# Gated linear attention inside a two-layer hybrid trunk: decay levels by products, one group of coupling products, full-size output products

## The chip, the cores and the metric

The kernel runs on one core of one Trainium2 chip. The metric is the device time of one execution in microseconds (us), as the median of several runs. TensorE is called PE in the profile (its weight loads PEld), VectorE DVE, ScalarE ACT, GpSimd POOL, SyncE SP. SP issues all transfers here.

## The reference, cut to what matters

A trunk of two layers over 2048 tokens of width 1024, all in float32. Each layer projects its input once and splits the columns between four heads of a gated delta rule (DeltaNet, "dn") and four heads of gated linear attention (GLA). Both groups are normalised by head, multiplied by a SiLU gate path, joined, projected back and added to the input before a layer norm. The change is in the GLA part, which computes, for keys of 64 channels and values of 128:

```python
# S_t = diag(exp(gk_t)) S_{t-1} + k_t v_t^T,   o_t = S_t^T q_t
log_f = jax.nn.log_sigmoid(gate_logits) / GLA_TAU          # GLA_TAU = 16, per token and key channel
Bc = jnp.cumsum(gc, axis=-2)                               # running log decay in a chunk
dec = jnp.where(causal, jnp.exp(diff), 0.0)                # diff = B_i - B_j, i >= j
attn = jnp.einsum("bhnid,bhnjd,bhnijd->bhnij", qc, kc, dec)
# over chunks:
o_n = einsum(q_n * exp(b_n), S) + einsum(a_n, v_n)
S = S * exp(b_last)[..., None] + einsum(k_n * exp(b_last - b_n), v_n)
```

The couplings `attn` can't be one matrix product, since the decay depends on the key channel too; and `q exp(B)` times `k exp(-B)` over a whole chunk would overflow.

## The kernel before

The work is done by layer and by half of the sequence (1024 tokens), so four times over. In each half the tokens come in two blocks of 512 (`b`), each of four chunks of 128 (`c`). Heads of GLA go in pairs (`p`): two heads of 64 key channels fill the 128 partitions, and `h` is the head in the pair. So there are four GLA blocks in a half, called (p, b) here, and 16 in all. DeltaNet has four heads by two blocks, eight blocks a half, numbered `n`.

A half runs in this order: transposes of the input (`prep_xt`) and token-major value projection (`proj_v`); the decay gates; the GLA blocks, with the projections for the next one (`gla_load`) between them; the DeltaNet keys (`keys_of`, `dn_keys`) one block ahead of the rest (`dn_rest`, which calls `dn_merge`); the gate paths (`gate`) strewn in between; the output projection with layer norm (`out_proj`). Projections (`proj_group`, L176 to L179) are products of 128 x 128 by 512 columns in a float32 form that is split in a high and a low part; 24 of them make one group of 128 channels for one block. The small products of GLA and DeltaNet are plain float32, each of which the profile counts as two instructions.

The order on each engine is fixed ahead of time by a scheduler that goes by priority (program order) and by its own estimate of durations; `issue_after` and `keep_in_program_order` are hints to it. Buffers come by tag, and a table (`SLOTS`, `BANKS`) says how many there are of each. Of the eight PSUM banks two are for projections ("pj"), three for transposes and couplings ("tr"), two for outputs ("ch") and one for merges ("mg").

The GLA block (`gla_block`) gets q and k, channels first, and the running log decay B from `gla_gates`, which sums it with a scan for each chunk (L331). To keep exponents small, it takes the couplings in levels: at level s, tokens of the second half of each stretch of 2s meet keys of the first half, both scaled by the decay to the border between the halves. Every level has its own subtraction from B, two exponentials on ACT and products on DVE. The levels 64, 32 and 16 (`LEVELS_BLOCK`) give whole blocks of the coupling matrix (L400); base blocks of 32 x 32 without decay come from L373; the levels 8, 4, 2 and 1 (`LEVELS_MASK`) come as 32 x 32 blocks, of which a mask picks the right entries (L439, L443). For these, q is laid out in a tile padded with zeros (`qpad`), so that one product with a contraction of 128 gives both heads. Then, chunk by chunk, an output product with the couplings A (L467, contraction 128), one with the state S (L468, contraction 64), the sum of squares on ACT, a copy on DVE, and the product that renews the state (L471), with the state itself on DVE (L472). `run_later` puts the transposes of the finished heads (`finish_head`) of the block before into the middle of the next.

SiLU and the exponentials need different tables on ACT. The gates of the first GLA head (`gla_gate(0)`) and the keys of DeltaNet's block 0 take a tanh form (`by_tanh`). DeltaNet's decay matrices (`dn_decay`) are exponentials too; they are written to DRAM and read back by `dn_keys`.

Of the kernel before, what the change touches and what calls it, by code (L numbers as in the profile page):

```python
# [9 lines left out]
F32 = mybir.dt.float32  # L10
# [3 lines left out]
ALU = mybir.AluOpType  # L14
# [15 lines left out]
SLOTS = {"xt": 4, "wh": 3, "wl": 3, "wr": 2, "oT": 10, "kT": 3, "kd": 3, "dec": 2, "U": 2, "Nn": 2, "lf": 2, "g4": 4,  # L30
# [8 lines left out]
def hymba_trunk(ctx: ExitStack, tc, x, w_in, conv_w, dn_a_log, dn_dt_bias, gla_gate_w2, gla_gate_b,  # L39
# [45 lines left out]
    # masks of the 32 x 32 diagonal blocks of the GLA couplings  # L85
# [21 lines left out]
    # starting rows of the triangular inversions: row 4 g + r of an identity at partition (g, chunk, block)  # L107
# [20 lines left out]
    cwh = C([P, 48], "cwh")  # L128
# [31 lines left out]
    later, anchor, tables = [], [], []  # L160
# [42 lines left out]
    def layer_params(l):  # L203
# [6 lines left out]
        nc.vector.tensor_scalar(out=cwh, in0=cw, scalar1=0.5, scalar2=None, op0=ALU.mult)  # L210
# [81 lines left out]
    def dn_decay(cums, n, decd):  # L292
        """Decay matrix of a block, transposed: exp(G_i - G_j) at [j, i], j <= i, with G the running log decay."""
# [6 lines left out]
        for c in range(NC):  # L300
            i = (b * NC + c) * 4 + h
            r = nc.scalar.activation(d[:, c, :], d[:, c, :], AF.Exp, bias=ngc[:, i:i + 1])
# [48 lines left out]

    def gla_block(p, qk, B, v, S):
        it = 1.0 / TAU
        qT, kT = qk
        B3 = B.rearrange("p (c t) -> p c t", c=NC)

        QE = T([P, BLK], "vb")
        EB = T([P, BLK], "y")
        anchor.append(nc.scalar.activation(EB, B, AF.Exp, scale=it))
        nc.vector.tensor_tensor(out=QE, in0=qT, in1=EB, op=ALU.mult)  # L360
        edec = small(NC, "edec")
        nc.vector.tensor_copy(edec, EB.rearrange("p (c t) -> p c t", c=NC)[:, :, P - 1])

        A = T([P, NC, 2, P], "g4")
        nc.gpsimd.memset(A, 0.0)
        banks = [PS([P, BLK], "tr") for _ in range(2)]
        d32 = [t[:, 0:256].rearrange("p (k c i) -> p k c i", k=2, c=NC) for t in banks]
        d64 = [t[0:64, 256:512].rearrange("p (c i) -> p c i", c=NC) for t in banks]
        for c in range(NC):
            for h in range(2):  # L370
                for j in range(0, P, 32):
                    r, cs = slice(64 * h, 64 * h + 64), slice(c * P + j, c * P + j + 32)
                    nc.tensor.matmul(d32[h][j:j + 32, 0, c, :], kT[r, cs], qT[r, cs], start=True, stop=True)  # L373

        def level(s):
            n = BLK // (2 * s)
            w = T([P, 515], "raw")[:, 0:BLK]
            w3 = w.rearrange("p (n t) -> p n t", n=n)
            Bn = B.rearrange("p (n t) -> p n t", n=n)
            nc.vector.tensor_tensor(out=w3, in0=Bn, in1=Bn[:, :, s - 1:s].to_broadcast([P, n, 2 * s]),  # L380
                                    op=ALU.subtract)
            nc.scalar.activation(w3[:, :, 0:s], w3[:, :, 0:s], AF.Exp, scale=-it)
            nc.scalar.activation(w3[:, :, s:], w3[:, :, s:], AF.Exp, scale=it)
            lv = T([P, BLK], "y")
            l3 = lv.rearrange("p (n t) -> p n t", n=n)
            nc.vector.tensor_tensor(out=l3[:, :, 0:s], in0=w3[:, :, 0:s],
                                    in1=kT.rearrange("p (n t) -> p n t", n=n)[:, :, 0:s], op=ALU.mult)
            nc.vector.tensor_tensor(out=l3[:, :, s:], in0=w3[:, :, s:],
                                    in1=qT.rearrange("p (n t) -> p n t", n=n)[:, :, s:], op=ALU.mult)
            return lv  # L390

        for s in LEVELS_BLOCK:
            lv = level(s)
            for c in range(NC):
                for h in range(2):
                    r = slice(64 * h, 64 * h + 64)
                    for j in range(0, P, 2 * s):
                        dst = (d64[h][:, c, :] if s == 64 else d32[h][j:j + s, 1, c, :] if s == 32
                               else d32[h][j:j + s, 0, c, s:])
                        nc.tensor.matmul(dst, lv[r, c * P + j:c * P + j + s], lv[r, c * P + j + s:c * P + j + 2 * s],  # L400
                                         start=True, stop=True)
        run_later()
        Ad = T([P, NC, 2, 32], "Y")
        for h in range(2):
# [5 lines left out]
        for s in LEVELS_MASK:  # L410
            n = BLK // (2 * s)
            q3 = qT.rearrange("p (n t) -> p n t", n=n)[:, :, s:]
            Bn = B.rearrange("p (n t) -> p n t", n=n)
            w = T([P, 515], "raw")[:, 0:BLK]
            if s > 1:
                w3 = w.rearrange("p (n t) -> p n t", n=n)
                nc.vector.tensor_tensor(out=w3, in0=Bn, in1=Bn[:, :, s - 1:s].to_broadcast([P, n, 2 * s]),
                                        op=ALU.subtract)
                nc.scalar.activation(w3[:, :, 0:s], w3[:, :, 0:s], AF.Exp, scale=-it)
                nc.scalar.activation(w3[:, :, s:], w3[:, :, s:], AF.Exp, scale=it)  # L420
                e3 = w3[:, :, s:]
                nc.vector.tensor_tensor(out=w3[:, :, 0:s], in0=w3[:, :, 0:s],
                                        in1=kT.rearrange("p (n t) -> p n t", n=n)[:, :, 0:s], op=ALU.mult)
# [30 lines left out]
        for c in range(NC):  # L454
            nc.tensor.transpose(pt[:, c, :], KE[:, c * P:(c + 1) * P], ident)
# [475 lines left out]
```

## Time and profile before

| | |
|---|---|
| median of 3 runs | 2501.54 us (2499.32 to 2502.89) |
| profiled execution, first to last instruction | 2508.8 us; no other time of that execution is listed |
| busy: PE, DVE, ACT, POOL | 2363.1, 1725.3, 1113.4, 327.6 us |
| mean granted PE clock | 0.964 |
| memory traffic | 157.84 MB read, 37.81 MB written |

The stages below are cut by hand at the lines that begin them: in the first half the GLA stage is 45 to 235 us from the start of the span and the DeltaNet stage 235 to 530; output projection and the next input follow to 665. A line of a group or of the timeline names the line of the kernel, the engine, the operation, the tile written and the tiles read, and the sizes. Matmuls overlap in the pipeline, so their lengths add up to more than the time that passes; the distance between two starts is what one costs. In tables by stretch of time each engine has its busy time and, in brackets, its instructions, and the last three columns are granted PE clock, DMA share and GB/s.

### The profile page before, as it was taken

The numbers are of one execution on the slowest core, as the hardware profiler recorded it, in microseconds if no ns is written. First come the engines' busy times: TensorE is split into PE (matmuls) and PEld (weight loads), VectorE is DVE, ScalarE is ACT, GpSimd is POOL, SyncE is SP. The second block draws the span as 40 slices with busy tenths as digits, with TensorE's granted clock in tenths as the row PEclk, the third lists the DMA queues.
The fourth block names the chain that finished last, engine by engine and source line by source line (L and its number), as shares of the span: only waits on it lengthen the run. The fifth ranks groups of instructions, "written<-read, shape, count | busy, mean of one in ns | idle before, by whom it ended". The sixth has DMA issues, their size and how long they took to land. (4 is left out here: it accounts for less than half of the span.)

```text
span 2508.8 us, 47498 instructions
## 1 busy us (share of the span) xinstructions
PE 2363.1 (94%) x17970; PEld 1891.7 (75%) x17970; DVE 1725.3 (69%) x4728; ACT 1113.4 (44%) x3149; POOL 327.6 (13%) x629
## 2 busy tenths in 40 slices
PE   8999999999999999989999989999999999999998
PEld 7776777788877677768887767777888877777777
DVE  4557777785556777777565678787766567777775
ACT  4654444451465444445146544444415654444440
POOL 2101111110010121111001012111100101211100
PEclk9999898999999999999999999999999999999999
DMA  4312121343321122144332122214433211222242
GB/s 140 83 35 68 50 74 33 94 148 101 117 70 53 50 60 65 34 99 144 102 118 69 53 51 60 65 37 105 145 99 116 78 45 42 64 60 54 75 133 80
DMA packets 242988, 198.72 MB, mean 79 GB/s; under 512 B 51972, under 2 KB 195656, under 8 KB 242760
## 3 DMA queue, kind: packets, MB, share of 16 engines
q1 hardware_dynamic: 242760, 195.70, 27.3%
q8 instruction: 141, 2.31, 0.4%
q14 instruction: 87, 0.71, 0.1%
HBM read 157.84 MB, written 37.81 MB: 78 GB/s over the span
## 5 line engine op out<-in xcount | busy, mean ns | idle before, releaser
L176 PE MATMUL pj<-xt,wh 128*128 128x512 f32 x1536 | 639.9, 417 | 2.0 <-ACT wh L152 2.0
L177 PE MATMUL pj<-xt,wh 128*128 128x512 f32 x1536 | 637.2, 415 | 0.0
L179 PE MATMUL pj<-xt,wl 128*128 128x512 f32 x1536 | 463.1, 424 | 0.0
L176 PEld LDWEIGHTS pj<-xt,wh 128*128 128x128 f32 x1536 | 298.4, 194 | 56.6 <-ACT wh L152 2.9
L177 PEld LDWEIGHTS pj<-xt,wh 128*128 128x128 f32 x1536 | 299.2, 195 | 54.9 <-issue 2.2
L179 PEld LDWEIGHTS pj<-xt,wl 128*128 128x128 f32 x1536 | 286.5, 198 | 53.1 <-issue 2.3
L490 DVE SCALAR_TENSOR_TENSOR y<-raw,cw,y 128x512 f32<-128x512 f32 x276 | 205.1, 743 | 29.0 <-ACT y L488 27.5
L745 PE MATMUL pj<-xt,wh 128*128 128x512 f32 x512 | 200.9, 392 | 0.0
L746 PE MATMUL pj<-xt,wh 128*128 128x512 f32 x512 | 200.3, 391 | 0.0
L152 ACT CAST wh<-wr 128x1024 fp32r<-128x1024 f32 (+2 forms) x116 | 118.6, 1023 | 158.5 <-PE pj L746 88.3
L154 DVE TENSOR_TENSOR wl<-wr,wh 128x1024 fp32r<-128x1024 f32 (+2 forms) x116 | 137.6, 1189 | 68.3 <-ACT wh L152 54.4
L698 POOL TENSOR_TENSOR ssd<-ssd,mhalf 128x1 f32<-128x1 f32 x128 | 87.1, 680 | 505.4 <-DVE ssd L697 505.0
L579 DVE TENSOR_TENSOR tmp<-Tb,g 128x64 f32<-128x64 f32 (+6 forms) x224 | 138.3, 617 | 3.0
L247 PE MATMUL pj<-wh,xt 128*128 128x280 f32 (+1 forms) x512 | 136.4, 297 | 0.0
L248 PE MATMUL pj<-wl,xt 128*128 128x280 f32 (+1 forms) x512 | 134.6, 294 | 0.9 <-issue 0.9
L748 PE MATMUL pj<-xt,wl 128*128 128x512 f32 x512 | 129.5, 391 | 0.0
L746 PEld LDWEIGHTS pj<-xt,wh 128*128 128x128 f32 x512 | 96.4, 188 | 19.2
L745 PEld LDWEIGHTS pj<-xt,wh 128*128 128x128 f32 x512 | 96.2, 188 | 19.2
L748 PEld LDWEIGHTS pj<-xt,wl 128*128 128x128 f32 x512 | 95.6, 188 | 19.2
L248 PEld LDWEIGHTS pj<-wl,xt 128*128 128x128 f32 x512 | 98.4, 192 | 2.0 <-issue 1.8
L247 PEld LDWEIGHTS pj<-wh,xt 128*128 128x128 f32 x512 | 98.4, 192 | 1.3 <-issue 0.7
L737 ACT CAST wh<-oT 128x128 fp32r<-128x128 f32 x128 | 30.2, 295 | 149.3 <-PE pj L746 140.4
(247 smaller groups left out, 4470.4 us busy)
## 6 DMA issues: line engine op xcount, KB each, us to landing
wr<-in_w_in_dram SPq DMA_DIRECT2D x104, 512.0 KB
g<-nd SPq DMA_DIRECT2D x32, 512.0 KB
g<-in_w_out_dram SPq DMA_DIRECT2D x32, 512.0 KB
g<-in_x_dram SPq DMA_DIRECT2D x16, 512.0 KB
dec<-gr SPq DMA_DIRECT2D x32, 256.0 KB
decd<-dec SPq DMA_DIRECT2D x32, 256.0 KB
dec<-decd SPq DMA_DIRECT2D x32, 256.0 KB
og<-oT SPq DMA_DIRECT2D x32, 256.0 KB
```

What stands on the lines that cost most here:

```text
L152: nc.scalar.copy(hi, raw)
L154: nc.vector.tensor_tensor(out=lo, in0=raw, in1=hi.bitcast(F32), op=ALU.subtract)
L176: nc.tensor.matmul(acc, hi[:, k, :], xh[:, k, :], start=(k == 0), stop=False)
L177: nc.tensor.matmul(acc, hi[:, k, :], xl[:, k, :], start=False, stop=False)
L179: nc.tensor.matmul(acc, lo[:, k, :], xh[:, k, :], start=False, stop=(k == KT - 1))
L247: nc.tensor.matmul(acc, xh[:, k, cs], ws[k][0], start=(k == 0), stop=False)
L248: nc.tensor.matmul(acc, xh[:, k, cs], ws[k][1], start=False, stop=False)
L490: nc.vector.scalar_tensor_tensor(out=y, in0=raw[:, k:k + BLK], scalar=w[:, 12 * k + grp:12 * k + grp + 1], in1=y, op0=ALU.mult, op1=ALU.add)
L579: nc.vector.tensor_tensor(out=tmp, in0=Tb[:, :, 0:w].unsqueeze(2).to_broadcast([P, 4, 4, w]), in1=NbT[:, w:w + 4, 0:w].unsqueeze(1).to_bro ...
L745: nc.tensor.matmul(acc, oh[:, k, :], wh[:, k, :], start=(k == 0), stop=False)
L746: nc.tensor.matmul(acc, oh[:, k, :], wl[:, k, :], start=False, stop=False)
L748: nc.tensor.matmul(acc, ol[:, k, :], wh[:, k, :], start=False, stop=(k == KT - 1))
```

## The change

It has five parts.

- `gla_gates` gives the forget factors f themselves (one more exponential) and no running sums. `span_decays` multiplies neighbours on POOL, so that `spans[s]` holds the decay over each stretch of s tokens. The levels are carried on: keys and queries scaled for level 2s come from those of level s, half of them multiplied by a span (DVE), the other half copied (ACT). The last step gives QE and KE, and `spans[128]` the chunk decay.
- All coupling products and the products that renew the state are issued after the last level, in one chain of order. The levels 8 to 1 are taken for one head at a time, with a contraction of 64. The states of all four chunks are worked out ahead (`Sall`).
- QE is a tile of two zero-padded halves, so that the product with the state has a contraction of 128. All 16 output products of a block come in a row, into two banks; squares and scaled copies are read from there.
- The tanh forms go away. One table load for SiLU is placed behind the last decay exponential, and every SiLU behind it; each decay exponential is placed behind the last.
- The second gate of GLA and the keys of DeltaNet's block 0 change places around the last GLA block. The gated outputs of the first two DeltaNet heads go to DRAM as well, and `split_o` reads six heads from there instead of four.

```diff
-SLOTS = {... "oT": 10, ... "g4": 4,
+SLOTS = {... "oT": 6, ... "g4": 4, "tt": 1, "lv": 2, "Sc": 3,
-    qpad = [C([P, NC, 2, 64], f"qpad{i}") for i in range(2)]
+    qpad = [C([P, 2, BLK], f"qpad{i}") for i in range(1)]
...
-            if n == 0 and c == 0:
-                issue_after(r, anchor[-1])
+            issue_after(r, anchor[-1])
+            anchor[-1] = r
...
-        B = T([P, BLK], "lf")
-        for c in range(NC):
-            cs = slice(c * P, (c + 1) * P)
-            nc.vector.tensor_tensor_scan(out=B[:, cs], data0=ones, data1=a[:, cs], initial=0.0,
-                                         op0=ALU.mult, op1=ALU.add)
-        return B
+        f = T([P, BLK], "lf")
+        anchor.append(nc.scalar.activation(f, a, AF.Exp, scale=1.0 / TAU))
+        return f
+
+    def span_decays(f):
+        t = T([P, BLK], "tt")
+        spans, o, prev = {1: f}, 0, f
+        for s in (2, 4, 8, 16, 32, 64, 128):
+            n = BLK // s
+            cur = t[:, o:o + n]
+            p2 = prev.rearrange("p (n t) -> p n t", t=2)
+            nc.gpsimd.tensor_tensor(out=cur, in0=p2[:, :, 0], in1=p2[:, :, 1], op=ALU.mult)
+            spans[s], o, prev = cur, o + n, cur
+        return spans
...
+        def double(k, q, s, kd, qd):
+            n = BLK // (2 * s)
+            sp = spans[s].rearrange("p (n t) -> p n t", t=2)
+            c = lambda t: t.rearrange("p (n t) -> p n t", n=n)
+            nc.vector.tensor_tensor(out=c(kd)[:, :, 0:s], in0=c(k)[:, :, 0:s],
+                                    in1=sp[:, :, 1:2].to_broadcast([P, n, s]), op=ALU.mult)
+            nc.scalar.copy(c(kd)[:, :, s:], c(k)[:, :, s:])
+            for r, d in qd:
+                nc.vector.tensor_tensor(out=c(d)[:, :, s:], in0=c(q)[r, :, s:],
+                                        in1=sp[r, :, 0:1].to_broadcast([r.stop - r.start, n, s]), op=ALU.mult)
+                nc.scalar.copy(c(d)[:, :, 0:s], c(q)[r, :, 0:s])
+
+        qs = T([P, BLK], "y")
+        nc.vector.tensor_tensor(out=qs, in0=qT, in1=f, op=ALU.mult)
+        lv = {1: (kT, qs)}
+        tags = {2: "y", 4: "Nn", 8: "U", 16: "raw", 32: "vb", 64: "lv"}
+        for s in (1, 2, 4, 8, 16, 32):
+            t = tags[2 * s]
...
+            double(*lv[s], s, kn, [(slice(0, P), qn)])
+            lv[2 * s] = kn, qn
+        KE = T([P, BLK], "at")
+        QE = qpad[0]
+        double(*lv[64], 64, KE, [(slice(64 * h, 64 * h + 64), QE[64 * h:64 * h + 64, h, :]) for h in range(2)])
...
+        pl = [PS([P, 4, NC, 16], t) for t in ("tr", "mg")]
...
+        pn = PS([P, NC, P], "ch")
+        def small_mm(*a):
+            m = nc.tensor.matmul(*a, start=True, stop=True)
+            if chain[0] is not None:
+                issue_after(m, chain[0])
+            chain[0] = m
+        for c in range(NC):
+            for h, r in enumerate(rows):
+                small_mm(pn[r, c, :], kend[:, c, r], v[:, c, h * P:(h + 1) * P])
         for s in LEVELS_BLOCK:
...
+                        if s == 16:
+                            small_mm(d32[h][j:j + 32, 0, c, :], kT[r, o:o + 32], qT[r, o:o + 32])
+                        small_mm(dst, kl[r, o:o + s], ql[r, o + s:o + 2 * s])
+        for m, s in enumerate(LEVELS_MASK):
+            kl, ql = lv[s]
+            for c in range(NC):
+                for j in range(0, P, 32):
+                    for h, r in enumerate(rows):
+                        o = c * P + j
+                        qh = ql[r, o:o + 32].rearrange("p (n t) -> p n t", t=2 * s)[:, :, s:]
+                        small_mm(pl[h][j:j + 32, m, c, :].rearrange("p (n t) -> p n t", t=s), kl[r, o:o + 32], qh)
         run_later()
+        Sall = [S] + [T([P, P], "Sc") for _ in range(NC - 1)]
...
+        po = [PS([P, 2, 2, P], "ch") for _ in range(2)]
+        for c in range(NC):
+            for h in range(2):
+                d = po[c // 2][:, c % 2, h, :]
+                nc.tensor.matmul(d, A[:, c, h, :], v[:, c, h * P:(h + 1) * P], start=True, stop=False)
+                nc.tensor.matmul(d, QE[:, h, c * P:(c + 1) * P], Sall[c], start=False, stop=True)
+                nc.scalar.activation(T([P, P], "sq", mybir.dt.bfloat16), d, AF.Square, scale=P ** -0.5,
+                                     accum_out=ssq[:, 2 * c + h:2 * c + h + 1])
...
-            for h in range(2):
-                r = slice(64 * h, 64 * h + 64)
-                po = PS([P, P], "ch")
-                nc.tensor.matmul(po, A[:, c, h, :], v[:, c, h * P:(h + 1) * P], start=True, stop=False)
-                nc.tensor.matmul(po, QE[r, cs], S[r, :], start=False, stop=True)
...
-                nc.vector.tensor_copy(os_[h][:, c, :], po)
-                nc.tensor.matmul(pn[r, :], kend[:, c, r], v[:, c, h * P:(h + 1) * P], start=True, stop=True)
...
+        issue_after(nc.scalar.activation(dst, y, AF.Silu), silus[-1])
...
-            og = [dr.tile([4, P, BLK], F32, ...
+            og = [dr.tile([6, P, BLK], F32, ...
...
-            keys_of(0)
+            silus.append(nc.scalar.preload_act_table_set("silu_and_others"))
+            issue_after(silus[-1], anchor[-1])
...
             gla_gate(0)
+            gla_gate(1)
             gla(1, 1)
-            gates_at = {0: (gla_gate, 1), 1: (gla_gate, 2), ...
+            keys_of(0)
+            gates_at = {1: (gla_gate, 2), ...
```

More of the change, by code (lines that the diff above doesn't have):

```diff
@@ L375, in level @@
[L375 to L390, printed above, removed]
+        rows = [slice(64 * h, 64 * h + 64) for h in range(2)]
@@ L403, in gla_block @@
         Ad = T([P, NC, 2, 32], "Y")
+        for c in range(NC - 1):
+            nc.vector.scalar_tensor_tensor(out=Sall[c + 1], in0=Sall[c], scalar=edec[:, c:c + 1], in1=pn[:, c, :],
+                                           op0=ALU.mult, op1=ALU.add)
         for h in range(2):
@@ L700, in dn_rest, with gate @@
         return o, gd
-    def gate(w, xtb, get, by_tanh=False):
+    def gate(w, xtb, get):
         acc = proj_group(w, xtb)
@@ L808, in hymba_trunk @@
             nc.gpsimd.memset(sm, 1.0)
-            og = [dr.tile([4, P, BLK], F32, tag=f"og{b}", name=f"og_{l}_{hf}_{b}", bufs=2) for b in range(NB)]
+            og = [dr.tile([6, P, BLK], F32, tag=f"og{b}", name=f"og_{l}_{hf}_{b}", bufs=2) for b in range(NB)]
             oTs = [[None] * NB for _ in range(4)]
@@ L870, in gla_gate @@
                     get = lambda: og_t[e // 2, b][e % 2]
-                    gate(w, xt[b], get, e == 0)
-                    nc.sync.dma_start(og[b][e], get())
+                    gate(w, xt[b], get)
+                    nc.sync.dma_start(og[b][2 + e], get())
             def dn_gate(hs, bs=range(NB)):
```

129 lines of the change are left out of this document (37 added, 92 removed).

## The prediction

> **What bounds the kernel now.** I read the page's busy table first, then a table by stage (busy time of each engine, last columns granted clock, DMA share, GB/s).
>
> ```profile
> span 2508.8 us, 47498 instructions
> PE 2363.1 (94%) x17970; PEld 1891.7 (75%) x17970; DVE 1725.3 (69%) x4728; ACT 1113.4 (44%) x3149; POOL 327.6 (13%) x629
> ...
> 45.00:235.00 190.00, 178.31 (x2053) 138.79 (x2053) 122.67 (x324) 109.92 (x311) 25.69 (x39) 0.97 0.24 63
> 235.00:530.00 295.00, 275.25 (x1669) 216.98 (x1668) 225.73 (x686) 130.97 (x378) 41.57 (x88) 0.95 0.26 68
> 665.00:853.00 188.00, 177.83 (x2057) 138.32 (x2056) 122.91 (x324) 109.99 (x311) 26.30 (x41) 0.97 0.23 64
> 1293.00:1480.00 187.00, 176.66 (x2051) 136.94 (x2050) 123.76 (x323) 108.62 (x309) 25.90 (x39) 0.98 0.22 64
> 1913.00:2101.00 188.00, 177.53 (x2056) 137.85 (x2055) 122.68 (x324) 109.93 (x311) 25.63 (x38) 0.98 0.23 64
> ```
>
> PE bounds every stage. The four GLA stages (one per layer and half, four blocks each, so 16 blocks) last 753 us together; PE is idle in 42.7 us of them, and the clock column (3, 3, 2, 2 per cent lost of some 188 us each) costs about 19 us more. The DeltaNet stage (second row) follows each: DVE is at 77% there.
>
> But a busy PE is not one at its pace. The timeline shows it: start, length, line, count of instructions; a float32 product is two instructions. What counts is the distance from start to start.
>
> ```profile
> 79.12 0.46 PE L467 MATMUL ch<-g,g 128*128 128x128 f32 x2
> 79.51 0.49 PE L468 MATMUL ch<-Sg,vb 64*128 64x128 f32 x2
> 79.93 0.49 PE L467 MATMUL ch<-g,g 128*128 128x128 f32 x2
> 80.35 0.49 PE L468 MATMUL ch<-Sg,vb 64*128 64x128 f32 x2
> 80.76 0.44 PE L471 MATMUL mg<-g,kd 128*64 128x128 f32 x4
> 81.13 0.40 PE L318 MATMUL tr<-ident,sm 128*50 128x128 f32 x2
> 81.37 0.39 PE L467 MATMUL ch<-g,g 128*128 128x128 f32 x2
> 81.59 0.27 PE L318 MATMUL tr<-ident,sm 128*50 128x128 f32 x1
> ...
> 82.21 0.43 PE L471 MATMUL mg<-g,kd 128*64 128x128 f32 x2
> 82.57 0.49 PE L467 MATMUL ch<-g,g 128*128 128x128 f32 x2
> ...
> 186.42 1.06 PE L543 MATMUL tr<-kT 128*128 128x128 f32 x8
> 187.24 0.47 PE L176 MATMUL pj<-xt,wh 128*128 128x512 f32 x1
> ```
>
> Four full products in a row (L543) take 0.82 us, 0.205 each. The output products of GLA, which go back and forth between a contraction of 128 (L467) and of 64 (L468), take 0.39 to 0.42 each; an L467 between full-size work takes 0.22 (81.37). One L471 product costs 0.36, two together 0.37.
>
> **The change, part by part.** (1) Output products. QE becomes a zero-padded 128-row tile, so L468's successor contracts over 128 and all 16 output products of a block are of one size. Of the old ones, eight L468 at 0.42 and eight L467 at about 0.33 (between 0.22 and 0.42) become 16 at 0.21: 6.0 - 3.4 = 2.6 us. The eight L471 products stand alone or in pairs (1.5 to 2.9 us, I take 2.1, the middle) and become one run: 0.36 and then about 0.1 each, 1.1. Together -3.6 us a block, -58 in 16 (between -42 and -64).
>
> (2) Coupling products. The levels 8, 4, 2, 1 lose the padded operand: 16 products of both heads become 32 of one head, 128 more instructions a block.
>
> ```profile
> 61.14 0.76 PE L373 MATMUL tr<-qT,kT 64*32 64x32 f32 x64 [0.80 <-ACT kT L349]
> 61.82 1.07 PE L400 MATMUL tr<-y 64*64 64x64 f32 x48
> 62.82 0.50 PE L177 MATMUL pj<-xt,wh 128*128 128x512 f32 x1
> ...
> 72.78 0.46 PE L439 MATMUL tr<-qpad,raw 128*32 128x32 f32 x32 [1.22 <-DVE qpad L435]
> 73.16 0.50 PE L179 MATMUL pj<-xt,wl 128*128 128x512 f32 x1
> ...
> 75.86 0.39 PE L176 MATMUL pj<-xt,wh 128*128 128x512 f32 x1
> 76.09 0.39 PE L177 MATMUL pj<-xt,wh 128*128 128x512 f32 x1
> 76.41 0.46 PE L439 MATMUL tr<-qpad,kT 128*32 128x32 f32 x32
> 76.79 0.50 PE L176 MATMUL pj<-xt,wh 128*128 128x512 f32 x1
> ```
>
> Before: 0.68 (L373) + 1.00 (levels 64, 32) + about 0.6 (level 16, at L373's pace) + 4 x 0.38 (L439) = 3.8 us. After, 432 instructions: 0.9 for levels 64 and 32, and 384 at between 8.4 ns (L439's 0.38 less 0.11, by 32) and 10.6 ns (L373's 0.68 by 64): 4.1 to 5.0; I take 4.5, +0.7 a block, +11. A rule speaks against this: the Trainium skill, "TensorE: Matmul & The Clock Gate", section "Wait — 56ns, not 53.3ns?", says that starts never come closer than about 25 ns. By it the 432 would take 10.8 us, and the sum would be about 2546; the trace does not agree, its 64 starts in 0.68 us are 10.6 ns apart.
>
> (3) Changes of size in between. A 512-wide product takes 0.23 (75.86 to 76.09), the one ahead of a small group 0.32, and the one after is as late. Some eight such visits a block become one or two: -1.2 us a block at 0.2 each, -19 (between -10 and -30).
>
> (4) Clock. Two pairs of consecutive 3.4 us windows, columns as in the table by stage:
>
> ```profile
> 63.60:67.00 3.40, 2.04 (x100) 1.45 (x100) 2.50 (x7) 1.79 (x8) 0.00 (x0) 1.00 0.21 74
> 67.00:70.40 3.40, 3.40 (x12) 2.73 (x9) 1.42 (x4) 1.13 (x4) 0.38 (x1) 0.50 0.92 131
> ...
> 251.30:254.70 3.40, 3.40 (x15) 2.35 (x14) 1.65 (x8) 0.51 (x2) 0.00 (x1) 0.50 0.02 5
> 254.70:258.10 3.40, 3.40 (x15) 3.11 (x14) 1.85 (x7) 0.00 (x0) 0.00 (x0) 0.50 0.00 0
> ```
>
> The first window has 1.36 us idle and many small products; the one after it runs at half clock, which costs 1.7 us where PE is the bound. The window from 251.3 is busy throughout, with 64 x 64 products in it, and still the next stays at half: small products seem to count little. The new group is some 5.5 us of them. I take one slow window a block: 27 us against 19, +9 (from -19 for none to +36 for two). The Trainium skill, "TensorE: Matmul & The Clock Gate", section "Why this matters for your kernels", names idle gaps over about 3 us as what drops the clock; by that the group would never do it, and the sum would be 2418. The trace differs: the half clock at 67.0 follows a window with only 1.36 us idle in all.
>
> (5) Idle PE in the GLA stages.
>
> ```profile
> PE tr L439 <- DVE qpad L435: 19.7, 19, 3.2
> PE mg L629 <- DVE U L626: 60.1, 24, 5.0
> ...
> L422 DVE TENSOR_TENSOR raw<-raw,kT 128x256 f32<-128x256 f32 x48 | 20.7, 432 | 12.5 <-ACT raw L419 12.2
> L446 ACT COPY g<-Y 32x256 f32<-32x256 f32 x32 | 12.9, 402 | 13.4 <-DVE Y L443 13.2
> L298 POOL TENSOR_SCALAR_AFFINE_SELECT dec<-dec 128x512 f32<-128x512 f32 x32 | 21.8, 684 | 187.3 <-DMA dec<-gr 185.2 <-ACT dec L302 1.1 <-ACT raw L419 0.9
> ...
> POOL dec L298 <- DMA dec<-gr: 185.2, 27, 26.3
> ```
>
> Now PE waits at each level in turn. After, the levels form one chain: a product of forget factors on POOL, then per level two DVE products of 256 (0.43 each) beside two ACT copies (0.40 each), about 1.1 us with the handover, seven levels: 8 us; then the KE transposes and 4.5 to 5.5 us of group. The level tiles hold both "raw" and all three "y" buffers until the group is done, so the next block's forget gates start only then. Gates of some 4 us, chain 8, group 6, masks and copies 4: 22 to 24 us, against the 188 / 4 = 47 us that a block has now. Cover: the next block's 48 projection products at 0.23, 10.9 us, and as much again from a value projection (96 products of half the width or a little more) or from the gates. Without this cover a block would cost some 10 us more. POOL's products have no row; the nearest is the 512-wide select at 0.68, so seven of 256 columns and fewer take up to 4.8 us, against 8 of the chain, and each must only be ahead of its own level: nothing. With 22 us of cover for a chain of 22 to 24 little should be open, but the order on PE is fixed ahead of time and may miss by a little at each of the two waits of a block (group, outputs): I take 60% of the idle time as left, -17 (from -40, none left, to +40, as much again). DVE loses four scans, eight subtractions and eight copies a block, ACT swaps its exponentials for as many copies; neither was the bound, so 0.
>
> All SiLUs now wait for one table load behind the last decay exponential, and these behind the forget factors of block (1,1). Queued behind on ACT are the gates, and on PE the third projection (two "pj" banks). The decays wait for DMA at worst 26.3 us (row above). 10.9 us of gate projection and the output products of (1,0) cover it: 0, at worst 10 a half. The extra stores of gated heads on SP and larger loads ahead of the output projection come early or in pairs of buffers: 0.
>
> (6) keys_of(0) moves behind the last GLA block, and the second gate ahead of it.
>
> ```profile
> 181.12 2.32 DVE L490 SCALAR_TENSOR_TENSOR y<-raw,cwh,y 128x512 f32<-128x512 f32 x3 [3.94 <-ACT y L488]
> 237.04 0.68 DVE L601 TENSOR_TENSOR U<-U,bd 128x512 f32<-128x512 f32 x1
> ```
>
> From its convolution to its inverse in use 56 us pass, beside the GLA block. After, with DVE freer, 40 to 50, and they start after the group. Cover on PE: GLA outputs 3.4, five further projections (24 products at 0.23, so 5.4 each), transposes and small products 5 or so: 35 us. I take 4.5 us idle a half, +18 (0 to +80).
>
> Sum: -58 + 11 - 19 + 9 - 17 + 18 = -56 us on the profiled span of 2508.8. That span is 7.3 us above the median of the runs, 0.3%, which changes no term; 2501.5 - 56 = 2445.
>
> **The rivals.** (A) The keys come too late, the end on the other side. If only k1, v0 and q0 get ahead of the merge (some 24 us of cover), 26 us are open in each half: 104 instead of 18, and the time is 2531. It decides from 18.5 us a half, where the other terms (-74) are used up. For it: PE already waits 60.1 us at L629 for this chain. Against: GLA no longer contends for DVE there. 0.13. (B) The group costs two slow windows and idle time stays: +27 + 17, 2489. For it the window of 251.3; against, only 3.4 us windows wholly inside the group can trigger. 0.15. (C) No slow window and no late keys: -27 - 18, 2400. For it: no idle gaps in the group. 0.17. (D) Full size does not bring 0.21, because the 0.42 comes from waiting for weights: +42, 2487. Against it L543. 0.04. (E) Products in the group come in pairs on the same part of the array (level 16 behind its base) and with gaps in their columns, and run at the pace of the 64-wide ones, 1.00 / 48 = 21 ns: 432 take 9.0 instead of 4.5, +72, 2517. For it that row; against, L373 and L439. 0.02.
>
> **How the numbers follow.** The forecast has 0.49, its own range is 2420 to 2475. The 80% range, 2388 to 2512, takes in B, C and D and leaves out A, E and a tail of C (0.13 + 0.02 + 0.04). A change under 0.2% can't be told from none. Slower: 0.16 (A, E, a tail of B). Same: 0.05 (B and D a little larger, A of half its size). Faster: 0.79.
>
> **What would show it.** Output products at 0.21 to 0.23 start to start, 16 in a row; the small group in 4 to 5.5 us without projections inside (8 or more speaks for E); one window at half clock after each group or none; PE waits ahead of the group and at the first merge of each half under 8 us. Wrong would make it a hole of over 18 us between the last GLA block and the first merge, or a GLA stage above 180 us.

## The result: slower by 4.7%, and the profile after

The changed kernel takes 2621.2 us (median; 2611.5 to 2628.1), the kernel before 2502.2 (2499.3 to 2503.6): a ratio of 1.0471, 95% interval 1.044 to 1.0501. Forecast were 2445 us, with a range of 2388 to 2512. The profiled execution took 2623.1 us, 0.1% above the median; its span is 2621.1 against 2508.8, so 112.3 us are to be found, and 168 from the forecast's -56.

First the page's head, busy time and the instruction queue (q8: packets, MB, share of 16 DMA engines):

```profile
span 2621.1 us, 51414 instructions
PE 2348.7 (90%) x20018; PEld 1920.5 (73%) x20018; DVE 1583.4 (60%) x4314; ACT 1092.8 (42%) x3129; POOL 331.4 (13%) x692
...
q8 instruction: 157, 2.57, 0.4%
```

PE is busy 14 us less than before, and the span is 112 longer: PE idles (272 us against 146) and its clock is lower. The q8 row, which the prediction passed over, is the key to the case. 20,018 products and as many weight loads make 40,036 instructions; in 157 packets that is 255 each, at 2.57 MB / 157 = 16 KB a packet. So I read the row as TensorE's instructions, which come from memory in blocks of 256; the experiments below bear it out.

The table by stage, with the columns of the prediction's table; the four GLA stages and the first DeltaNet stage:

```profile
45.00:247.00 202.00, 176.34 (x2591) 147.56 (x2592) 77.48 (x197) 106.33 (x315) 29.78 (x54) 0.92 0.23 63
247.00:558.00 311.00, 277.17 (x1718) 218.28 (x1717) 242.08 (x725) 135.32 (x384) 38.84 (x89) 0.94 0.30 75
690.00:894.00 204.00, 174.78 (x2590) 145.94 (x2588) 75.91 (x195) 105.86 (x314) 30.34 (x56) 0.92 0.22 62
1342.00:1546.00 204.00, 173.65 (x2587) 145.12 (x2586) 75.25 (x192) 105.18 (x311) 29.55 (x53) 0.92 0.22 61
2001.00:2198.00 197.00, 172.60 (x2588) 144.80 (x2587) 75.70 (x193) 105.41 (x312) 29.26 (x53) 0.93 0.23 64
```

GLA: 807 us against 753. PE is busy 697 of them, against 710, although the second gate (10.9 us a half, 44 in all) came in: the work did get some 57 us shorter. But PE idles 110 us in place of 43, and a clock of 0.92 to 0.93 costs about 63 us in place of 19 (part of it under idle time). DeltaNet's stage lost the gate's 10.9 us and is longer all the same, 311 against 295, with 34 us idle against 20.

What PE waited for (total, times, longest; L407 is every coupling and state product):

```profile
PE mg L621 <- DVE U L618: 67.4, 24, 5.2
PE tr L407 <- issue: 52.2, 25, 2.8
PE tr L643 <- ACT qT L489: 26.6, 20, 3.1
PE mg L407 <- issue: 26.6, 12, 2.7
PE mg L605 <- DVE Nd L599: 26.0, 22, 3.7
```

37 waits, 78.8 us, end with "issue": PE waited for nothing that the profile shows as a producer. The merge (first row, 60.1 before) is 7 us worse. L643 and L605, in DeltaNet, have grown by 22 and 23 us; the kernel before has for the same code:

```profile
PE tr L651 <- ACT qT L497: 4.4, 6, 1.0
...
PE mg L613 <- DVE Nd L607: 2.9, 12, 0.6
```

Now one group, that of block (1,1), in the timeline:

```profile
208.74 1.09 PE L407 MATMUL ch<-g,kd 128*64 128x128 f32 x16
209.77 0.68 PE L407 MATMUL tr<-lv,lv 64*64 64x64 f32 x16
...
214.33 0.20 PE L407 MATMUL tr<-U,U 64*32 64x16 f32 x1 [1.85 <-issue]
218.33 0.23 PE L407 MATMUL tr<-y,y 64*32 64x16 f32 x1 [2.75 <-issue]
```

And the same group in a table of stretches cut at the pauses, for L407 alone (length, PE, weight loads, then clock, DMA share, GB/s):

```profile
208.74:214.30 5.56, 3.74 (x245) 3.40 (x245) 1.00 0.01 3
214.30:218.30 4.00, 1.25 (x128) 1.15 (x128) 0.74 0.01 4
218.30:219.22 0.92, 0.89 (x75) 0.85 (x75) 0.50 0.00 0
```

The group lasts 10.5 us where 4.5 for the couplings and 1.1 for the state products were forecast. Between the two pauses stand exactly 128 products with 128 weight loads: one block of 256 instructions, run in 1.25 us; then PE has nothing until the next comes. And the first pause lies in the middle of level 8, at no border of the computation. The columns DMA and GB/s of the same 12 us (40 slices of 0.3 us):

```profile
GB/s 0 0 0 0 0 0 0 0 0 0 0 0 0 55 0 0 0 0 0 0 0 0 0 0 0 0 55 0 0 0 0 0 0 0 0 0 0 0 0 55
...
q8 instruction: 3, 0.05, 1.6%
```

Three packets move, all of the instruction queue, at 211.9, 215.8 and 219.7, and PE goes on 2.4 and 2.5 us after each of the first two began. The output products, as forecast:

```profile
227.30 0.39 PE L462 MATMUL ch<-Sc,qpad 128*128 128x128 f32 x2
227.52 0.39 PE L461 MATMUL ch<-g,g 128*128 128x128 f32 x2
227.75 0.39 PE L462 MATMUL ch<-Sc,qpad 128*128 128x128 f32 x2
227.97 0.39 PE L535 MATMUL tr<-kT 128*128 128x128 f32 x2
```

From start to start 0.22 each, against 0.39 to 0.42. They don't stand 16 in a row, as the prediction's sign had it: projections and transposes still come in between, here after every second or fourth.

### The profile page after: what moved, and what is told of

Its sections match the earlier page's. It is cut to its first block, busy times and chain, and to the rows that moved or that the text cites. A ratio compares the mean times of both kernels' runs of the same rounds, so it can differ in the third digit from the quotient of the medians.

```text
span 2621.1 us, 51414 instructions
## 1 busy us (share of the span) xinstructions
PE 2348.7 (90%) x20018; PEld 1920.5 (73%) x20018; DVE 1583.4 (60%) x4314; ACT 1092.8 (42%) x3129; POOL 331.4 (13%) x692
## 3 DMA queue, kind: packets, MB, share of 16 engines
q8 instruction: 157, 2.57, 0.4%
## 4 chain that ended last, share of the span: by engine, by line
PE 53%; DVE 19%; DMA 13%; issue 6%; ACT 6%; POOL 2%; SPq 0%; DVEq 0%; ACTq 0%; POOLq 0%
DMA g<-nd 8%; PE pj L178 5%; PE pj L175 5%; PE pj L176 5%; PE pj L733 5%; PE pj L734 5%; PE pj L736 4%; DVE tmp L571 3%; DMA nd<-Nd 3%; DVE y L486 3%; PE tr L407 2%; PE pj L248 2%; PE pj L246 2%; PE pj L245 2%; DVE R L574 1%
## 5 line engine op out<-in xcount | busy, mean ns | idle before, releaser
L175 PE MATMUL pj<-xt,wh 128*128 128x512 f32 x1536 | 634.0, 413 | 10.6 <-ACT y L699 8.6
L178 PE MATMUL pj<-xt,wl 128*128 128x512 f32 x1536 | 438.8, 409 | 0.0
L486 DVE SCALAR_TENSOR_TENSOR y<-raw,cw,y 128x512 f32<-128x512 f32 x288 | 214.8, 746 | 33.1 <-ACT y L484 30.6
L736 PE MATMUL pj<-xt,wl 128*128 128x512 f32 x512 | 130.0, 392 | 0.0
L574 DVE TENSOR_REDUCE R<-tmp 128x16 f32<-128x64 f32 (+6 forms) x224 | 92.9, 415 | 3.3
```

Source lines behind the costliest of these rows:

```text
L175: nc.tensor.matmul(acc, hi[:, k, :], xh[:, k, :], start=(k == 0), stop=False)
L178: nc.tensor.matmul(acc, lo[:, k, :], xh[:, k, :], start=False, stop=(k == KT - 1))
L486: nc.vector.scalar_tensor_tensor(out=y, in0=raw[:, k:k + BLK], scalar=w[:, 12 * k + grp:12 * k + grp + 1], in1=y, op0=ALU.mult, op1=ALU.add)
L736: nc.tensor.matmul(acc, ol[:, k, :], wh[:, k, :], start=False, stop=(k == KT - 1))
```

## The experiments

Times are medians; the kernel before gave 2494.8 to 2502.2 in the different sets, so differences between sets are good to some 7 us. e1 and e5 were measured in one execution each. Two theories were open for the group: that its instructions come too slowly, or that the pauses are ordinary waits which the trace names badly. And for DeltaNet: late keys, or the gate taken out of it.

**e1: half the instructions.** `kT`, `qT`, `qs`, `kn`, `qn` become tiles of `mybir.dt.bfloat16`; nothing else.

> q, k and the level tiles of GLA are bfloat16, so the couplings are rounded; a coupling product is then one TensorE instruction (and one weight load) in place of two, with the number and size of the products as before. Theory S (the group waits for its instructions: they come in blocks of 256, one about every 3.6 us, and a group has 896): the group has 464 instructions, at most one pause is left in it, the group takes 3 to 5 us in place of 10.4, the waits of the coupling line for 'issue' fall from 79 us to under 20, and the time is 2510 to 2550. Rival W (the pauses are waits for data, banks or array parts that the trace names badly): as many products wait in the same way, pauses as long as before, 2590 to 2625. Rival F (a floor of some 25 ns from start to start): 232 starts spread evenly over 5.8 us without pauses, about 2550.

2519.2 us in one execution, 102 less. The products are the same, their instructions are half. Waits of PE, and the queue on the page:

```profile
PE tr L407 <- issue: 10.7, 5, 2.3
PE mg L407 <- issue: 10.5, 5, 2.2
```

```profile
q8 instruction: 130, 2.13, 0.4%
```

The waits for issue fall from 78.8 to 21.2, ten in place of 37. Theory S as expected, with 21 where under 20 stood. The 102 us are more than the 58 of waits: idle time of PE falls by 62 us (272.4 to 210.4), and its busy time by 42 (2348.7 to 2306.8), since half of the couplings' instructions are gone and the mean clock is 0.946 in place of 0.936. So e1 shows what the waits hang on, not what they alone cost.

**e2: levels asked for one by one.** `couple(s)` issues the products of level s.

```diff
-        for s in LEVELS_BLOCK:
...
-        for m, s in enumerate(LEVELS_MASK):
...
+        couple(1)
         for s in (1, 2, 4, 8, 16, 32):
             double(*lv[s], s, kn, [(slice(0, P), qn)])
             lv[2 * s] = kn, qn
+            couple(2 * s)
```

> The changed kernel, with the coupling products of each level asked for as soon as its tiles are there, level 1 first and the state products last, instead of all in one group at the end; nothing else. Theory S: instructions are fetched while projections run in between, so the waits for 'issue' fall from 79 us to under 25 and the half-clock windows become fewer; changes of size between small and 512-wide products come back (some 14 more a block at 0.15, +34). 2540 to 2590. Rival W: the pauses stay with the products, and the changes of size come on top: 2620 to 2660. Rival F: evenly spaced starts, hidden nowhere, 2600 to 2640.

2606.8 us (1.0416, interval 1.0382 to 1.0451), 14 less, with 86 us of waits for issue. The time is that of rival F, but its evenly spaced starts are not there: 40 pauses of 2.2 us on average are; between S and W nothing is decided, and as an experiment it failed. In the timeline all the levels stand in one run again; the scheduler did not part them. It needs a forced order (e7).

**e5: the supply by itself.** Bursts of small products between projection-sized ones.

> No GLA at all, the output is zero: bursts of small products with 64 projection-sized products (14.7 us) before, between and after. In order: 64, 128, 256 and 512 float32 products of 64x32 by 32; 512 bfloat16 ones of the same size; 128 float32 ones of 128x128 by 128; 256 float32 ones of 64x64 by 64. A float32 product is two products and two weight loads, a bfloat16 one is one of each. Theory S (blocks of 256 instructions, one per about 3.6 us once what lies ready is used up): 1.4 us without a pause; 2.7 to 5 with one pause at most; 8 to 12 with two or three; 23 to 28 with some seven; the 512 bfloat16 ones as the 256 float32 ones, 8 to 12; the 128-wide ones 26 us without a pause; the 64-wide ones 11 to 14. Theory F (25 ns from start to start): 3.2, 6.4, 12.8, 25.6 and 12.8 us, evenly spaced, no pauses. Theory W (the pauses belong to the GLA block's data): 1.4, 2.7, 5.4, 10.8 and 5.4 us, no pauses.

The table of stretches, cut at the pauses (length, PE busy and products, weight loads, DVE and POOL, which have none, then clock, DMA share, GB/s): 64 float32 products; 128 and the projection-sized ones behind them; 256; part of 512; part of 512 in bfloat16; 64-wide ones.

```profile
20.98:22.20 1.22, 1.22 (x129) 1.18 (x128) 0.00 (x0) 0.00 (x0) 1.00 0.05 13
36.96:40.90 3.94, 2.07 (x224) 1.97 (x224) 0.00 (x0) 0.00 (x0) 1.00 0.02 4
40.90:41.27 0.37, 0.33 (x34) 0.25 (x33) 0.00 (x0) 0.00 (x0) 1.00 0.00 0
41.27:44.70 3.43, 3.43 (x15) 2.72 (x11) 0.00 (x0) 0.00 (x0) 0.63 0.02 5
44.70:48.10 3.40, 3.40 (x15) 2.73 (x14) 0.00 (x0) 0.00 (x0) 0.87 0.00 0
...
57.64:61.20 3.56, 1.54 (x160) 1.44 (x160) 0.00 (x0) 0.00 (x0) 1.00 0.02 5
61.20:64.70 3.50, 1.28 (x128) 1.18 (x128) 0.00 (x0) 0.00 (x0) 0.70 0.02 5
64.70:68.15 3.45, 1.53 (x128) 1.42 (x128) 0.00 (x0) 0.00 (x0) 0.50 0.02 5
68.15:69.33 1.18, 1.15 (x97) 1.09 (x96) 0.00 (x0) 0.00 (x0) 0.50 0.07 14
...
97.60:101.05 3.45, 1.54 (x128) 1.42 (x128) 0.00 (x0) 0.00 (x0) 0.50 0.02 5
...
133.60:137.05 3.45, 1.20 (x128) 1.10 (x128) 0.00 (x0) 0.00 (x0) 0.60 0.02 5
...
200.86:215.93 15.07, 15.07 (x513) 15.01 (x512) 0.00 (x0) 0.00 (x0) 1.00 0.02 4
```

1.2 us without a pause; 4.3 with one; 11.7 with three; the 512 float32 ones 26.9 and the 512 bfloat16 ones 12.1, as the 256 float32 ones of as many instructions. Every stretch from one pause to the next holds 128 products, of either type, and a new one begins each 3.45 to 4.0 us, with 4 to 5 GB/s of traffic in all. What lies ready when a burst begins is 159 to 223 products, 318 to 446 instructions. F falls (starts come 8 to 10 ns apart within a block), W falls (no GLA here). The 64-wide products start 29 ns apart from the first to the last, those that lay ready included: that is a pace of their own. At it 128 take 3.7 us, about as long as the supply needs for them, and they show no pause (15.1 us, expected 11 to 14).

**e7: order forced in half of the blocks.** As e2, but `chain` also runs through pieces of eight projection products of the next block, put between the levels in blocks (0,0) and (1,0).

> The kernel of e2_spread with the order on TensorE forced in half of the blocks, (0,0) and (1,0): between the levels stand eight projection products each of the next block's q and k (six pieces, 1.9 us each). The other blocks are as in e2_spread. Theory S: a filled block spreads its 896 instructions over some 16 us, 256 per 4 us, so it has no pause for 'issue', and the waits for 'issue' fall from 86 us to some 45, all of it in the unfilled blocks. With six more changes of size (about 0.3 us each) and fewer half-clock windows the time falls by 20 to 50 us from 2607: 2555 to 2590. Rival W: pauses in both kinds of blocks, over 75 us of waits, 2600 to 2630.

Waits of PE at the small products:

```profile
PE tr L404 <- issue: 39.0, 18, 3.7
PE ch L404 <- ACT kd L456: 25.7, 8, 3.6
PE mg L404 <- issue: 7.3, 3, 3.0
```

Waits for issue 46.3 in place of 86.1; in the timeline all of them lie in the eight unfilled blocks, two or three in each, none in the filled ones. S holds for the cause. The time does not follow: 2603.1 us (1.0416, 1.0374 to 1.0458) where 2555 to 2590 were expected. The state products were chained behind the pieces, too, and PE now stands still for the transposed keys (`kd`), eight times 3.2 us; changes of size may do the rest, which was not measured.

**e3 and e6: keys and gate.** e3 puts `keys_of(0)` ahead of `gla(1, 1)` and the second gate to DeltaNet's block 0, with other buffers for level 4; e6 moves only the gate.

> The changed kernel with the keys of DeltaNet's block 0 ahead of the last GLA block again and the second gate behind DeltaNet's block 0 again (the level-4 tiles of GLA get other buffers, so that this is possible). Theory C (from its first keys to its last merge DeltaNet is one chain of DVE and DMA, and what starts later ends later): the first merge comes 10 to 20 us earlier in each half, the waits at the merges of the first and the last block shrink, and the time falls by 40 to 70 us to 2550 to 2580. Rival T (TensorE has the same work in any order, and the lost time is in the GLA blocks alone): 2610 to 2625.

2661.9 us (1.0649, 1.0605 to 1.0692): neither theory. My edit made its own wait: one of the level-4 tiles shares a buffer with DeltaNet's inversion, and PE waited for the levels behind it (waits of PE, 23 us a half):

```profile
PE tr L407 <- DVE lv L373: 92.4, 4, 23.3
```

Less these 92 us it would be 2570, as theory C says, but that is argued, not shown; e11 makes the test without the shared buffer.

> The changed kernel with one thing undone: the second gate stands behind DeltaNet's block 0 again; the keys stay where the change put them. Theory G (DeltaNet's blocks are paced by their chain on DVE, ACT and DMA, and a projection that is taken out of them leaves a hole): the GLA stage gets 10 us a half shorter and DeltaNet's stage hardly longer, so 2576 to 2595. Rival K (the holes of DeltaNet come from keys that start late, wherever the gate is): without the gate in front the first merge waits even longer, and the time is 2610 to 2650.

2595.8 us (1.0392, 1.0357 to 1.0427), 25 less, at the edge of what G gives; K falls. The gate alone is a fifth of the loss: 44 us of work taken out of DeltaNet's stages did not shorten them by as much. L643 and L605, the rows that had grown, fall to 13.7 and 5.4 us although the keys are still late, and L495, the transposes of the keys, rises from 3.4 to 25.2.

**e8 and e11: keys and gate together.** e8 is e1 and e11 is e2, each with the order below. Level 4 gets buffers of its own in e8; in e11 the levels 4, 16, 32 and 64 change buffers.

```diff
-            gla_gate(1)
-            gla(1, 1)
             keys_of(0)
-            gates_at = {1: (gla_gate, 2), 2: (gla_gate, 3), 3: (dn_gate, [0]), 5: (dn_gate, [1])}
+            gla(1, 1)
+            gates_at = {0: (gla_gate, 1), 1: (gla_gate, 2), 2: (gla_gate, 3), 3: (dn_gate, [0]), 5: (dn_gate, [1])}
```

> The kernel of e1_bf16 (q, k and level tiles of GLA in bfloat16) with the keys of DeltaNet's block 0 ahead of the last GLA block and the second gate behind DeltaNet's block 0, as before the change; level 4 has buffers of its own, so no wait as in e3_keys. Theory C (chain of DeltaNet, started earlier, with the gate to fill it): 10 to 17 us a half less than 2519, most of it at the first merge and after the last: 2452 to 2480, faster than the kernel before. Rival T (only the GLA blocks lost time): 2505 to 2525.

> The kernel of e2_spread with keys of DeltaNet's block 0 and the second gate as before the change, nothing forced and nothing rounded. Theory C: 42 us less than e2_spread as from e1 to e8, 2555 to 2580, with the waits for 'issue' unchanged at 75 to 95. Theory T (the keys matter only once the groups are short): 2595 to 2610.

e8: 2476.7 us (0.9903, 0.9876 to 0.993), 42 less than the one execution of e1 and 1% faster than the kernel before. (One of its ten executions took 7407.8 us, for no reason that a trace shows; without it the median is 2476.5.) e11: 2546.3 us (1.0195, 1.0152 to 1.0237), 60 less than e2, more than the 27 to 52 expected, with the waits for issue as they were. Theory C in both. The waits of DeltaNet that had come with the change, in e2:

```profile
PE tr L645 <- ACT qT L491: 30.7, 20, 3.1
...
PE mg L607 <- DVE Nd L601: 24.1, 18, 3.7
```

And in e11, where the other is no longer listed:

```profile
PE tr L645 <- ACT qT L491: 6.0, 8, 1.3
```

So with late keys and without the gate PE has, block after block, its projections done and DeltaNet's chain not there yet. How much of it the keys cost and how much the gate is not shown: these two runs move both, and the gate alone had already shrunk these rows (e6).

**e4 and e12: the output products alone.** The kernel before, with q in a 128-row padded tile (e4), and with the state products in one run ahead of the outputs as well (e12).

```diff
-                nc.tensor.matmul(po, QE[r, cs], S[r, :], start=False, stop=True)
+                nc.tensor.matmul(po, QE[:, h, cs], S, start=False, stop=True)
```

> The kernel before with one part of the change: the decayed q in a zero-padded tile of 128 rows for each head, so that the output product with the state contracts over 128; the state products stay in between, and there are 8 buffers for finished heads in place of 10. By the prediction's first term the state outputs cost 0.21 in place of 0.42 and the others 0.22 to 0.25 in place of 0.33, the state products as before: 2.0 to 2.8 us a block, -32 to -45, so 2457 to 2470. Rival D (the cost is that of a change between lines, not of size): 2495 to 2505.

> The kernel of e4_before_full with the eight state products of a block in one run ahead of the output products, into one bank. By the traces a state product costs 0.29 us between outputs of another size (9.2 us for 32 in a half of e4) and 0.13 in a run (1.02 for 8 in the changed kernel), so 1.3 us a block, and the output products stand next to each other: -20 to -28, 2452 to 2462. Rival B (the products wait for the transposed keys and hold up the outputs, or the bank that they keep holds up the next block): 2475 to 2490.

e4: 2479.4 us (0.9909, 0.9872 to 0.9946), less gain than the 32 to 45 expected, but rival D falls. e12: 2476.9 (0.992, 0.9891 to 0.9948), the time of rival B, but not its wait: the outputs wait for the copies that free their banks, not for the keys. PE is busy 2363.1 us before, 2336.2 in e4 and 2312.8 in e12, and idle 145.7, 146.2 and 162.0. How long the level products wait for DVE, in the kernel before:

```profile
PE tr L400 <- DVE y L388: 7.7, 12, 1.1
```

In e4:

```profile
PE tr L404 <- DVE y L392: 22.5, 16, 4.2
```

And in e12, where the outputs (L475) wait as well:

```profile
PE tr L404 <- DVE y L392: 21.4, 16, 4.1
...
PE ch L475 <- DVE o L478: 9.7, 17, 2.2
```

In e4 this wait is made up for by others (the wait for `qpad` falls from 19.7 to 11.1), and the gain is small because the outputs, with state products still between them, cost 0.27 us each from start to start, against 0.36 before and 0.22 in the changed kernel. In e12 PE's gain of another 23 us becomes 16 us of idle time. I read it so that faster products reach the next level earlier and DVE is not done with it; no run tests this.

**e9 and e10: order forced everywhere, state products free.** As e7, in all blocks, with larger pieces: in e9 for the bfloat16 kernel e8, in e10 for float32.

> The kernel of e8_bf16_keys, with the coupling products asked for level by level and parted on TensorE by force in every block: levels 1 to 8 (256 instructions), then 24 projection products that are needed anyway (of q and k, of the value projection or of the first gate), then levels 16, 32 and 64 (176 instructions); the state products stand free. Theory S: neither part is longer than what lies ready, so the waits for 'issue' fall from 27 us to under 5 and some half-clock windows go with them; one more pair of changes of size a block costs 6 us: 2440 to 2462. Rival O (the forced order only moves the wait to what comes next in the block, as the 25.7 us for the transposed keys in e7_filler): 2470 to 2495.

> The same with float32 tiles as in the changed kernel, so exact: levels 1 and 2, 4 and 8, 16, 32 and 64 in four parts (up to 256 instructions each) with up to 16 projection products between them (24 half-wide ones in block (0,1)), keys and second gate placed as before the change. Theories S and C together: 2607 (e2_spread) less 42 (keys and gate, from e1 to e8) less some 75 (waits for 'issue', 86 to under 15) less some 15 (clock), plus 19 (three more visits a block at 0.4): 2494, within 2470 to 2520. Rival O: the waits come back at another line, 2530 to 2565.

Waits for issue at the coupling products: none in e9 (26.7 in e8), 3.8 us in e10 (72.4 in e11). Times: 2484.7 (0.9955, 0.9922 to 0.9988) and 2547.0 (1.0201, 1.0152 to 1.025), no better than e8 and e11. Rival O in both. In their place stand, in e9:

```profile
PE tr L533 <- ACT kT L527: 32.0, 8, 6.0
PE tr L412 <- ACT raw L400: 23.9, 8, 3.1
```

And in e10:

```profile
PE ch L469 <- ACT kd L465: 24.2, 12, 3.3
PE ch L499 <- DVE g L492: 21.8, 4, 7.0
```

In these two runs a fixed order traded a wait for instructions for waits on data that the scheduler had hidden.

**e13: fewer instructions instead.** e8 with the levels 8 to 1 for both heads at once, from a padded q, as before the change:

```diff
-                    for h, r in enumerate(rows):
...
-                        small_mm(pl[h][j:j + 32, m, c, :].rearrange("p (n t) -> p n t", t=s), kl[r, o:o + 32], qh)
+                    small_mm(pl[j:j + 32, m, c, :, :], kl[:, c * P + j:c * P + j + 32], qm[s][:, c, :, j // 2:j // 2 + 16])
```

> The kernel of e8_bf16_keys (bfloat16 couplings, keys and second gate as before the change) with the couplings of the levels 8, 4, 2 and 1 taken for both heads at once from a zero-padded q, as before the change: 64 products fewer, so a group has 336 instructions in place of 464; eight small copies a block on DVE and POOL come with it, and half of the masked copies go. Theory S (the last of the lost time is the 27 us of pauses left, and the half-clock windows behind them): 318 to 446 instructions lie ready in e5_burst, so a pause stays in a few blocks only, waits for 'issue' under 8 us, 2440 to 2462. Rival R (the rest is elsewhere): waits for 'issue' fall all the same and the time stays at 2468 to 2485. Rival L (the copies make the level chain longer and TensorE waits for it): 2480 to 2500.

2444.9 us (0.9789, 0.9761 to 0.9816), the fastest of all and 1.8 to 2.4% faster than the kernel before. From its page:

```profile
PE 2257.0 (92%) x15538; PEld 1831.8 (75%) x15538; DVE 1590.9 (65%) x4314; ACT 1101.3 (45%) x3129; POOL 411.1 (17%) x760
```

And its waits for issue at the coupling products:

```profile
PE tr L420 <- issue: 5.2, 3, 2.5
```

Theory S: three pauses in 16 groups, and most groups take 2.5 us. Its price is that the couplings are taken from bfloat16 tiles.

## Why the prediction was wrong, step by step

The direction was wrong because of two steps: the coupling products, whose pauses also slowed the clock, and DeltaNet's cover (step 6 and the gate). Steps 1 and 5 held.

- **Step 2, coupling products: the step that failed.** The pace of 8.4 to 10.6 ns a start was right inside a block (e5). What was left out is that it was read from runs of 64, 48 and 32 instructions, and carried over to one of 432. The page showed q8, and e5 shows its price: beyond the 318 to 446 instructions that lie ready, 256 come in 3.45 to 4.0 us. 448 product instructions with their loads are 896, so each group waits two or three times. 10.5 us in place of 5.6; 78.8 us of waits in all. The text said that 8 us or more would speak for rival E (a pace of 21 ns): the length did, the mechanism was another. Its sign "a GLA stage above 180 us" was badly set, since the second gate alone adds 10.9 to a stage.
- **The rule weighed in step 2** (the Trainium skill, "TensorE: Matmul & The Clock Gate", starts never closer than about 25 ns) gave 2546, nearer than my 2445, and the trace did not bear out its reason: starts are 8 to 10 ns apart, with pauses. For the group alone its result came near (10.8 us), since 128 products in 3.45 to 4.0 us is 27 to 31 ns each. The prediction did not use the page of the Trainium skill that bears on the cause, "Runtime: NRT & Kernel Launch", section "Instruction fetch mechanics", which says that instructions come in blocks of 256 through a queue of their own. The Trainium skill says there too that this is hidden behind the issue floor; here a block is used up in 1.2 to 1.5 us and the next takes 3.45 to 4.0, so it is not.
- **Step 4, clock: +9 forecast, about +44 measured** (63 against 19). One slow window a block was taken, and small products were suspected. In e5 the clock stays at 1.00 through 15 us of 64-wide products and through the 64 float32 ones; it drops to 0.5 in the stretches behind pauses of some 2 us. In the GLA groups, too, the windows follow the pauses, and these come from step 2: rival B's price, for another reason.
- **Step 6 and the gate: +18 forecast for the keys, nothing for the gate.** The step's own figures, 40 to 50 us of chain against 35 of cover, leave 5 to 15 us a half open, 20 to 60 in all, not 18. Moving both back gave 42 us (e8) and 60 (e11), the gate alone 25 (e6). The gate's 10.9 us a half were counted as cover for the decays in GLA and not as cover lost in DeltaNet. Rival A had the place right; it was not the one large hole ahead of the first merge, but many waits of 1.2 to 1.3 us on average, 3.7 at most (L643, L605).
- **Step 1, outputs: right on PE.** 0.22 each and 16 state instructions in 1.03 us. From start to start over the whole trace the outputs and state products cost 126 us before and 74 after, 53 less where 58 stood. (The 1.5 to 2.9 us named for the state products would give bounds of -48 and -70, not -42 and -64.) In the kernel before a part of the gain became idle time once the state products stood in one run as well (e12).
- **Step 5, other idle time in GLA: about right.** Without the pauses the GLA stages idle 31 us against 43, forecast -17. **Step 3** could not be sized apart: a projection product's mean mixes size changes with slow windows.

The balance: e1, e8 and e13 give back 102, 42 and 32 us, together the 176 between measurement and forecast, and e13 stands at the 2445 forecast. That the numbers meet so closely is partly chance: e1 was measured once, these kernels also halve the couplings' instructions on PE and (e13) the masked copies on DVE, and no exact float32 version got below 2546 with the new levels. In float32 the waits for issue went from 72.4 us (e11) to 3.8 (e10) and the time stayed, 2546.3 and 2547.0. So the cause of the pauses is shown; what they alone cost in the end is not.

## What to carry to other kernels

Count TensorE's instructions, weight loads and the second pass of float32 included, wherever many small products run together, and look at the instruction queue in the profile: beyond some 300 to 450 in a row they came here at 256 in 3.45 to 4.0 us. Fewer instructions (one for two heads, one pass in place of two) helped; a forced order between them only moved the wait. And work that is taken out of a stage with a long chain takes that chain's cover with it: cost it there, not only where it goes.

## What the runs showed of the hardware that was not expected

- One pause of 1.9 us is followed by some 3.4 us at half clock: behind the burst of 128 in e5 the clock is 0.63 and 0.87 in two stretches of 3.4 us (41.27, 44.70), which is 1.7 us lost. In the group at 208.74 it is 0.74 and 0.50 behind the first pause. The Trainium skill, "TensorE: Matmul & The Clock Gate", section "Why this matters for your kernels", names gaps above about 3 us; the pauses here are shorter.
- At half clock the supply of instructions keeps its pace: 128 products in 3.45 us at 0.50 (64.70 and 97.60 in e5), in 3.50 at 0.70 (61.20). In these rows it depends neither on the clock nor on the operands' type (bfloat16 at 133.60: 3.45).
